# Second-half squares, row statistics and operand sums placed elsewhere at the begin of each stage of a two-layer encoder

## The chip, the cores and the metric

The kernel runs on one core of a Trainium2 chip. The metric is the device time of one execution in microseconds (us). Three runs of the kernel before are shown, and one profiled execution from which all rows below come.

## The reference

The reference is a trunk of two layers over 1024 tokens of 1024 channels in float32. Each layer has two stages that begin with a root-mean-square norm: a mixer and a feed-forward block.

```python
for l in range(DEPTH):
    h = rmsnorm(x, attn_norm_g[l])
    x = x + hybrid_mixer(h, w_in[l], ...)     # h @ w_in, then three branches, then w_out
    h = rmsnorm(x, ffn_norm_g[l])
    x = x + conv_ffn(h, w_up[l], ffn_conv_w[l], w_down[l])
return rmsnorm(x, final_norm_g)
```

What matters here is the first product of each stage: the normed `h` times a wide matrix, `w_in` (6912 columns) or `w_up` (4096 columns). A norm needs, for each token, the sum over all channels of x squared; its inverse root scales the token, and a gain scales the channel.

## The kernel before

**Layout.** Channels lie on the 128 partitions, tokens along a row. The activations come in two halves of 512 tokens; each half is four tiles (parts 0 to 3), and a tile holds two pieces of 128 x 512: channel block k and block k + 4. The first half's tiles are `x_i_0_j` at the first stage and `x_o_0_0_j` at the second, the second half's `x_i_1_j` and `x_o_0_1_j`, with j the part. Two flat operations on a piece (512 elements a partition) are the unit of almost all of VectorE's and ScalarE's work.

**Products.** Each float32 operand is held as a high and a low piece in a shorter format: ScalarE casts the high one, VectorE subtracts it from the operand for the low one. For weights that is `split_to` (L287, L288), for activations `halves` (L346, L347). A product of 128 x 128 weights and 512 tokens is then three matmuls (high by high, high by low, low by high), all at L337. Tiles `split_n` come from a pool of five buffers, so a weight cast waits until the matmuls of the weights five places back are over. Sums of weight quarters (`s1` to `s4`) are made by DMAs ahead of time and split in the same way.

**Blocks.** A `Block` makes two output tiles of 128 channels by 1024 tokens with seven products in place of eight, by sums of quarters. With b11 and b21 the first half's channel blocks 0 to 3 and 4 to 7, and b12 and b22 the second half's, the operands of activations are B11 = b11, B21 = b21, t3 = b12 - b22 (T3), T1 = b11 - b12, T2 = t3 - b11, T4 = b21 + T2, and B22 = b22. Each has four parts of 128 channels, and a product with one operand is twelve matmuls. `first()` makes B11 into the bank `run` (copied by ScalarE to p1, L381) and B21 into the bank `c11`, and VectorE adds both to z1 (L363). `second()` adds T2's product to `run`, which ScalarE copies to u2 (L391). `rest()` makes T3's product in the bank `c21`, which ScalarE copies to p7 (L401); then T1's on top of `run`, T4's on top of `c21` (so not before p7 is copied), and B22's on top of `run`.

**A stage's begin.** Four times (m_0, f_0, m_1 and f_1: mixer and feed-forward block of layers 0 and 1) `start_phase` begins a stage. Four blocks run their `first()` from the first half alone. Meanwhile the second half's row statistics are made: the sum of squares (squares by ScalarE, L477; sums by VectorE, L363), a product with ones (`st`, L422), the power on GpSimd (L429), a diagonal on VectorE (L439) and its product with ones (`r`, L452). Then VectorE norms the second half's eight pieces (L485) and makes t3, T1 and T2 in place; T2's and T3's pieces are cast and split; the four blocks run their `second()`; and T1, T4 and B22 follow. At m_0 alone there is nothing ahead of the begin: x is loaded, the first half's squares summed and its tiles normed, while the second half's tiles land. At the other three the last product of the stage before runs meanwhile.

**What sets the order.** The kernel is traced from the top, and a scheduler of the framework, when the program is built, places the instructions of every engine by its own estimate of when each can run. What the kernel text fixes is the order of what depends on each other, and `tc.issue_after(ins)`, which puts the instructions traced inside the block behind `ins` on the engine of `ins`. On the chip, every engine takes its rows in the built order, and a row that waits holds what stands behind it.

Of the kernel before, what the change touches and what calls it, by code (L numbers as in the profile page):

```python
# [10 lines left out]
AF = mybir.ActivationFunctionType  # L11
ALU = mybir.AluOpType

P = 128
D = 1024
S = 1024
L = 2
H = 512
NH = S // H
DB = 768  # L20
KD = D // P
# [51 lines left out]
C_NG = C_PS + KB  # L73
# [29 lines left out]
def encoder(ctx: ExitStack, tc: tile.TileContext, xt, wts, par, bs, wst, cnt, out):  # L103
    nc = tc.nc
# [9 lines left out]
    def slot(name):  # L114

        return up.tile([P, 2, H], F32R, tag="u", name=name)
# [5 lines left out]
    def temp(name):  # L122
        return wp.tile([P, H], F32, tag="t", name=name, bufs=N_TT)
# [63 lines left out]
    state = {"raw": 0, "split": 0, "used": 0, "dma": None, "credit": 0, "pow": None}  # L187
# [156 lines left out]
    def halves(u, f):  # L344

        nc.scalar.copy(u[:, 0], f)  # L346
        nc.vector.tensor_tensor(u[:, 1], f, u[:, 0].bitcast(F32), op=ALU.subtract)  # L347

    def split_slot(name, f):
        u = slot(name)  # L350
        halves(u, f)
        return u
# [7 lines left out]
        nc.vector.tensor_tensor(u[:, 1], whole_of(u), u[:, 0].bitcast(F32), op=ALU.subtract)  # L360

    def add(o, a, b, op=ALU.add):
        nc.vector.tensor_tensor(o, a, b, op=op)  # L363

    class Block:

# [80 lines left out]
    def rsqrt_rows(parts_of, name):  # L447

        dg, nc_ = parts_of
        r = pst.tile([P, H], F32, tag="st", name=f"r_{name}")  # L450
        for j in range(2):
            nc.tensor.matmul(r[:, :nc_], ones_r, dg[:, j, :nc_], start=j == 0, stop=j == 1)  # L452
        return r
# [17 lines left out]
    def x_part(xq, k):  # L471
        return xq[k % 4][:, k // 4]

    def square(sq, xq, k, cols, name):

        s = temp(f"sq_{name}_{k}")
        nc.scalar.activation(s[:, cols], x_part(xq, k)[:, cols], AF.Square)  # L477
        if sq is None:
            return s
        add(sq[:, cols], sq[:, cols], s[:, cols])  # L480
        return sq

    def normed_tile(xq, r, l, col, k):
        f = x_part(xq, k)
        nc.vector.scalar_tensor_tensor(  # L485
            f, f, parts[l][:, col + k : col + k + 1], r, op0=ALU.mult, op1=ALU.mult
        )

    def normed(xq, r, l, col):
        for k in range(KD):  # L490
            normed_tile(xq, r, l, col, k)
# [10 lines left out]
    def start_phase(l, col, x0, x1, sq1, name, ops, blocks, late):  # L502


        at = 2 if late else 1
        for b in blocks[:at]:
            b.first()
        rows = rsqrt_sums(sq1, 0, H, D, f"{name}_1")
        blocks[at].first()
        r = rsqrt_rows(rows, f"{name}_1")  # L510
        for b in blocks[at + 1 :]:
            b.first()
        t3 = []
        ops["T2"] = []
        for j in range(4):
            b11, b12, b22 = x_part(x0, j), x_part(x1, j), x_part(x1, j + 4)
            for k in (j, j + 4):
                normed_tile(x1, r, l, col, k)
            t3.append(temp(f"t3_{name}_{j}"))
            add(t3[j], b12, b22, ALU.subtract)  # L520
            add(b12, b11, b12, ALU.subtract)
            add(b11, t3[j], b11, ALU.subtract)
            ops["T2"].append(split_slot(f"T2_{name}_{j}", b11))
        ops["T3"] = [split_slot(f"T3_{name}_{j}", t3[j]) for j in range(4)]
        for b in blocks:
            b.second()
        ops["T1"] = [split_slot(f"T1_{name}_{j}", x_part(x1, j)) for j in range(4)]
        ops["T4"] = []
        for j in range(4):
            b21 = x_part(x0, j + 4)  # L530
            add(b21, b21, x_part(x0, j))
            ops["T4"].append(split_slot(f"T4_{name}_{j}", b21))
        ops["B22"] = [split_slot(f"B22_{name}_{j}", x_part(x1, j + 4)) for j in range(4)]
# [38 lines left out]
    def mixer_in(l, x0, x1, sq1, ops):  # L572
# [96 lines left out]
        def block(n):  # L669
            kind, j = IN_BLOCKS[n]  # L670
            return Block(l, *in_tiles(kind, j), ops, f"{kind}_{tag}_{j}")
# [26 lines left out]
                    nc.sync.dma_start(d[kind][c], z)  # L698

        blocks = [block(n) for n in range(EARLY)]  # L700
        start_phase(l, C_NG, x0, x1, sq1, f"m_{l}", ops, blocks, l == 0)
        for n in range(len(IN_BLOCKS)):
            if n >= EARLY:

                rate = PUMP[0] if n < len(IN_BLOCKS) - 6 else LAST_PUMP
                b = block(n)
# [7 lines left out]
            else:  # L714
                b, rate = blocks[n], PUMP[0]
# [224 lines left out]
        return x0, x1, sq1, ops  # L940

    def first_half(l, col, x0, sq0, name):
        normed(x0, rsqrt_rows(rsqrt_sums(sq0, 0, H, D, f"{name}_0"), f"{name}_0"), l, col)
        return first_operands(x0, name)


# [138 lines left out]
    x0 = x_load(xt, 0, "i_0", gated=False)  # L1085
    nc.sync.dma_start(parts[0], par[0])
    load_to(3)
    x1 = x_load(xt, 1, "i_1", gated=False)
    warm = sm.tile([P, 1], F32, tag="warm", name="warm", bufs=1)
    nc.scalar.activation(warm, ones[:, 0:1], AF.Sigmoid)  # L1090
    sq0 = sq1 = None
    for k in range(KD):
        sq0 = square(sq0, x0, k % 2 * 4 + k // 2, slice(0, H), "m_0_0")
    ops = first_half(0, C_NG, x0, sq0, "m_0")
    for k in range(KD):
        sq1 = square(sq1, x1, k % 2 * 4 + k // 2, slice(0, H), "m_0_1")
    later.append(lambda: nc.sync.dma_start(cnt_sb, cnt))
    for l in range(1, L):
        later.append(lambda l=l: nc.sync.dma_start(parts[l], par[l]))
    for l in range(L):  # L1100
        x_src = xt if l == 0 else x_dram[2 * l - 1]
        d = mixer_in(l, x0, x1, sq1, ops)
        x0, x1, sq1, ops = mixer_out(l, d, x_src, x_dram[2 * l])
        if l + 1 < L:
            x0, x1, sq1, ops = ffn(l, x0, x1, sq1, ops, x_dram[2 * l], x_dram[2 * l + 1])
# [96 lines left out]
```

## Time and profile before

| | |
|---|---|
| median of three runs (lowest, highest) | 2721.48 us (2721.25, 2721.61) |
| the profiled execution's own time | 2721.56 us |
| its span | 2719.7 us |
| mean granted TensorE clock | 0.998 |
| TensorE (PE) busy | 2671.9 us, 98% |
| TensorE's weight loads (PEld) busy | 2206.4 us, 81% |
| VectorE (DVE) busy | 2058.4 us, 76% |
| ScalarE (ACT) busy | 1254.6 us, 46% |
| GpSimd (POOL) busy | 370.2 us, 14% |

A row of a time line has the start in us from the span's begin, the duration from the first to the last of the instructions it merges, the engine, the line of the kernel, the operation, the tile written and those read, the size, and how often; in brackets the idle time before it and what ended it. Buffer numbers are left out of tile names there: `x_o` stands for all tiles of both halves, `T_f` for T1 to T4 at f_0 and f_1, `c_up` for c11 and c21, `run_up` for the bank `run`, `z_up` and `upv` for a block's two outputs, `p_up` for p1 and p7. A row of waits has the engine and its operation, what it waited for, the total, the number of times and the longest. A row of windows has the stretch, then busy time and number of instructions for PE, PEld, DVE, ACT and POOL, the granted share of TensorE's clock, the mean busy share of the DMA engines and what they moved.

### The profile page before, as it was taken

How to read it: one execution, taken by the hardware profiler on the slowest of the kernel's cores; microseconds unless marked ns; L12 is line 12 of the kernel's file. 1: busy time of each engine (PE TensorE's matmuls, PEld its weight loads, DVE VectorE, ACT ScalarE, POOL GpSimd, SP SyncE). 2: the span in 40 equal slices, each digit the busy share in tenths (PEclk: the TensorE clock that was granted, in tenths of full speed). 3: DMA queues.
4: the chain of work that ended last, by engine and by line, in shares of the span. 5: the costliest groups of instructions: out<-in, count | busy, mean ns of one | idle time of the engine just before them, and what ended most of it. 6: DMA issues, size and time to landing. Idle time of an engine off the chain costs nothing.

```text
span 2719.7 us, 35012 instructions
## 1 busy us (share of the span) xinstructions
PE 2671.9 (98%) x12122; PEld 2206.4 (81%) x12122; DVE 2058.4 (76%) x2879; ACT 1254.6 (46%) x2047; POOL 370.2 (14%) x423
## 2 busy tenths in 40 slices
PE   6999999999999999999999999999999999999998
PEld 4888888888888788878888888888888888888788
DVE  7997998967756976664579988898776579666656
ACT  5645444444333554553355444444442336445434
POOL 3231112100001311100122211110000022211000
PEclk9999999999999999999999999999999999999999
DMA  9888878673357787656569778786624677774654
GB/s 241 200 221 209 214 196 215 174 267 139 122 184 201 174 204 182 164 195 204 150 154 223 202 209 225 199 208 225 217 92 142 217 177 183 194 186 112 218 180 136
DMA packets 273923, 513.72 MB, mean 189 GB/s; under 512 B 28368, under 2 KB 49616, under 8 KB 273744
## 3 DMA queue, kind: packets, MB, share of 16 engines
q1 hardware_dynamic: 219120, 411.32, 45.7%
q0 software_dynamic: 54624, 100.16, 22.4%
q8 instruction: 95, 1.56, 0.2%
q14 instruction: 84, 0.69, 0.1%
HBM read 383.44 MB, written 87.03 MB: 173 GB/s over the span
## 4 chain that ended last, share of the span: by engine, by line
PE 81%; issue 13%; DVE 3%; DMA 2%; ACT 1%; POOL 0%; SPq 0%; DVEq 0%; POOLq 0%; ACTq 0%
PE run_up L337 13%; PE pd L337 12%; PE run_gate L337 10%; PE c_up L337 9%; PE c_gate L337 7%; PE run_glu L337 5%; PE ph L337 4%; PE c_glu L337 4%; PE po L337 3%; PE run_zp L337 2%; PE run_u L337 2%; PE run_v L337 2%; PE c_u L337 2%; PE c_zp L337 2%; PE c_v L337 1%
## 5 line engine op out<-in xcount | busy, mean ns | idle before, releaser
L288 DVE TENSOR_TENSOR split<-raw,split 128x512 fp32r<-128x512 f32 (+1 forms) x570 | 376.6, 665 | 254.5 <-ACT split L287 251.3
L287 ACT CAST split<-raw 128x512 fp32r<-128x512 f32 (+1 forms) x570 | 342.8, 603 | 465.1 <-PE pd L337 146.1
L595 DVE SCALAR_TENSOR_TENSOR conv<-z_glu,par,conv 128x1011 f32<-128x1011 f32 (+7 forms) x360 | 452.5, 1264 | 7.3 <-ACT conv L593 4.5
L287 ACT CAST split<-s 128x512 fp32r<-128x512 f32 x344 | 213.5, 622 | 368.6 <-issue 127.2
L337 PE MATMUL pd<-h,split 128*128 128x512 f32 (+1 forms) x1536 | 314.7, 364 | 3.7 <-ACT split L287 1.5
L337 PEld LDWEIGHTS pd<-h,split 128*128 128x128 f32 x1536 | 262.2, 189 | 51.9 <-ACT h L359 3.5
L288 DVE TENSOR_TENSOR split<-s,split 128x512 fp32r<-128x512 f32 x344 | 235.1, 686 | 65.0 <-ACT split L287 64.6
L219 POOL DMA_DIRECT2D s<-in_wts_dram x220 | 205.9, 977 | 400.0 <-DMA s<-in_wts_dram 182.2
L219 POOL DMA_DIRECT2D s<-s x156 | 136.7, 876 | 765.3 <-DMA s<-in_wts_dram 409.4
L337 PE MATMUL run_up<-T_f,split 128*128 128x512 f32 x768 | 184.5, 389 | 2.5 <-ACT T_f L346 2.5
L337 PE MATMUL run_up<-B_f,split 128*128 128x512 f32 x768 | 183.4, 393 | 2.5 <-DVE upv L363 2.5
L337 PE MATMUL c_up<-T_f,split 128*128 128x512 f32 x768 | 183.8, 389 | 0.3 <-ACT p_up L401 0.3
L337 PE MATMUL po<-y,split 128*128 128x512 f32 x768 | 175.7, 389 | 0.0
L337 PEld LDWEIGHTS run_up<-B_f,split 128*128 128x128 f32 x768 | 144.2, 189 | 34.8 <-DVE upv L363 4.7
L337 PEld LDWEIGHTS run_up<-T_f,split 128*128 128x128 f32 x768 | 143.8, 188 | 33.4 <-ACT T_f L346 3.5
L337 PEld LDWEIGHTS c_up<-T_f,split 128*128 128x128 f32 x768 | 144.0, 188 | 31.1 <-ACT p_up L401 1.2
L337 PEld LDWEIGHTS po<-y,split 128*128 128x128 f32 x768 | 144.0, 188 | 29.8
L337 PE MATMUL c_gate<-T_m,split 128*128 128x512 f32 x576 | 138.6, 389 | 0.0
L337 PE MATMUL run_gate<-T_m,split 128*128 128x512 f32 x576 | 138.5, 389 | 0.0
L337 PE MATMUL run_gate<-B_m,split 128*128 128x512 f32 x576 | 136.3, 389 | 0.0
L337 PE MATMUL ph<-mixed,split 128*128 128x512 f32 x576 | 136.1, 394 | 0.0
L337 PE MATMUL ph<-us,split 128*128 128x512 f32 x576 | 134.2, 391 | 0.0
(265 smaller groups left out, 4375.2 us busy)
## 6 DMA issues: line engine op xcount, KB each, us to landing
raw<-in_wts_dram SPq DMA_DIRECT2D x518, 256.0 KB, 3.4
s<-in_wts_dram SPq DMA_DIRECT2D x344, 256.0 KB, 3.6
s<-in_wts_dram POOLq DMA_DIRECT2D x220, 256.0 KB, 5.2
s<-s POOLq DMA_DIRECT2D x156, 256.0 KB, 4.2
gate<-z_gate SPq DMA_DIRECT2D x48, 512.0 KB, 4.2
gt<-gate SPq DMA_DIRECT2D x96, 256.0 KB, 3.7
h<-hd SPq DMA_DIRECT2D x56, 256.0 KB, 4.9
pooled_b<-poold SPq DMA_DIRECT2D x24, 512.0 KB, 10.0
```

What stands on the lines that cost most here:

```text
L219: nc.gpsimd.dma_start(s, o, accum_op=ALU.add)
L287: nc.scalar.copy(s[:, 0, :cols], src[:, :cols])
L288: nc.vector.tensor_tensor(s[:, 1, :cols], src[:, :cols], s[:, 0, :cols].bitcast(F32), op=ALU.subtract)
L337: nc.tensor.matmul(ps[:, cols], w[:, i0, wsl], a[:, i1, cols], start=first and k == 0 and j == 0, stop=last and k == n - 1 and j == 2, ski ...
L595: nc.vector.scalar_tensor_tensor(acc[:, k:], ain[:, : S - k], col(w0 - k), acc[:, k:], op0=ALU.mult, op1=ALU.add,)
```

## The change

Three edits, none of which changes what is computed.

- At m_0 the second half's squares are traced ahead of the first half's norm, and the first half's normed tiles are issued behind the sixth square on ScalarE and behind the fifth sum on VectorE (`issue_after(seen[0])`, `issue_after(seen[1])`).
- At m_0 the second half's statistics are traced behind the first block (`late` is now False), as at the other begins; it was behind the second block.
- At all four begins the second half's operand sums are made part by part: VectorE's rows of part j + 1 (two normed tiles, t3, T1, T2 and T2's low piece) are issued behind part j's last difference, T2's.

```diff
--- before.py
+++ after.py
@@ -360,7 +360,7 @@
         nc.vector.tensor_tensor(u[:, 1], whole_of(u), u[:, 0].bitcast(F32), op=ALU.subtract)
 
     def add(o, a, b, op=ALU.add):
-        nc.vector.tensor_tensor(o, a, b, op=op)
+        return nc.vector.tensor_tensor(o, a, b, op=op)
 
     class Block:
 
@@ -474,10 +474,10 @@
     def square(sq, xq, k, cols, name):
 
         s = temp(f"sq_{name}_{k}")
-        nc.scalar.activation(s[:, cols], x_part(xq, k)[:, cols], AF.Square)
+        state["squared"] = nc.scalar.activation(s[:, cols], x_part(xq, k)[:, cols], AF.Square).ins
         if sq is None:
             return s
-        add(sq[:, cols], sq[:, cols], s[:, cols])
+        state["summed"] = add(sq[:, cols], sq[:, cols], s[:, cols]).ins
         return sq
 
     def normed_tile(xq, r, l, col, k):
@@ -512,15 +512,20 @@
             b.first()
         t3 = []
         ops["T2"] = []
+        behind = None
         for j in range(4):
             b11, b12, b22 = x_part(x0, j), x_part(x1, j), x_part(x1, j + 4)
-            for k in (j, j + 4):
-                normed_tile(x1, r, l, col, k)
-            t3.append(temp(f"t3_{name}_{j}"))
-            add(t3[j], b12, b22, ALU.subtract)
-            add(b12, b11, b12, ALU.subtract)
-            add(b11, t3[j], b11, ALU.subtract)
-            ops["T2"].append(split_slot(f"T2_{name}_{j}", b11))
+
+            with ExitStack() as order:
+                if behind is not None:
+                    order.enter_context(tc.issue_after(behind))
+                for k in (j, j + 4):
+                    normed_tile(x1, r, l, col, k)
+                t3.append(temp(f"t3_{name}_{j}"))
+                add(t3[j], b12, b22, ALU.subtract)
+                add(b12, b11, b12, ALU.subtract)
+                behind = add(b11, t3[j], b11, ALU.subtract).ins
+                ops["T2"].append(split_slot(f"T2_{name}_{j}", b11))
         ops["T3"] = [split_slot(f"T3_{name}_{j}", t3[j]) for j in range(4)]
         for b in blocks:
             b.second()
@@ -698,7 +703,7 @@
                     nc.sync.dma_start(d[kind][c], z)
 
         blocks = [block(n) for n in range(EARLY)]
-        start_phase(l, C_NG, x0, x1, sq1, f"m_{l}", ops, blocks, l == 0)
+        start_phase(l, C_NG, x0, x1, sq1, f"m_{l}", ops, blocks, False)
         for n in range(len(IN_BLOCKS)):
             if n >= EARLY:
 
@@ -940,7 +945,9 @@
         return x0, x1, sq1, ops
 
     def first_half(l, col, x0, sq0, name):
-        normed(x0, rsqrt_rows(rsqrt_sums(sq0, 0, H, D, f"{name}_0"), f"{name}_0"), l, col)
+        if not isinstance(sq0, tuple):
+            sq0 = rsqrt_sums(sq0, 0, H, D, f"{name}_0")
+        normed(x0, rsqrt_rows(sq0, f"{name}_0"), l, col)
         return first_operands(x0, name)
 
 
@@ -1091,9 +1098,15 @@
     sq0 = sq1 = None
     for k in range(KD):
         sq0 = square(sq0, x0, k % 2 * 4 + k // 2, slice(0, H), "m_0_0")
-    ops = first_half(0, C_NG, x0, sq0, "m_0")
+    rows0 = rsqrt_sums(sq0, 0, H, D, "m_0_0")
+    seen = None
     for k in range(KD):
         sq1 = square(sq1, x1, k % 2 * 4 + k // 2, slice(0, H), "m_0_1")
+        if k == KD - 3:
+            seen = state["squared"], state["summed"]
+
+    with tc.issue_after(seen[0]), tc.issue_after(seen[1]):
+        ops = first_half(0, C_NG, x0, rows0, "m_0")
     later.append(lambda: nc.sync.dma_start(cnt_sb, cnt))
     for l in range(1, L):
         later.append(lambda l=l: nc.sync.dma_start(parts[l], par[l]))
```

The built order, at the three places that the prediction speaks of. First VectorE at f_0, just ahead of the first T2 product. `x_o_0_0_j` is part j of the first half, `x_o_0_1_j` of the second; a normed tile is at L485, `z1_up_0_2` and `z1_up_0_3` are outputs of the third and fourth block, `split` rows are weights. Before:

```order
L485 SCALAR_TENSOR_TENSOR x_o_0_1_2_6965<-x_o_0_1_2_6965,par_0_78,r_f_0_1_7465 128x512
L363 TENSOR_TENSOR z1_up_0_2_7468<-c11_up_0_2_7489,p1_up_0_2_7487 128x512
L288 TENSOR_TENSOR split_283_7536<-s2_0_92_7267,split_283_7536 128x512
L485 SCALAR_TENSOR_TENSOR x_o_0_1_3_6967<-x_o_0_1_3_6967,par_0_78,r_f_0_1_7465 128x512 x2
L363 TENSOR_TENSOR t3_f_0_0_7554<-x_o_0_1_0_6961 128x512
L363 TENSOR_TENSOR t3_f_0_1_7563<-x_o_0_1_1_6963 128x512
L363 TENSOR_TENSOR x_o_0_1_0_6961<-x_o_0_0_0_6634,x_o_0_1_0_6961 128x512
L363 TENSOR_TENSOR x_o_0_1_1_6963<-x_o_0_0_1_6636,x_o_0_1_1_6963 128x512
L363 TENSOR_TENSOR x_o_0_0_0_6634<-t3_f_0_0_7554,x_o_0_0_0_6634 128x512
L363 TENSOR_TENSOR z1_up_0_3_7516<-c11_up_0_3_7535,p1_up_0_3_7533 128x512
L363 TENSOR_TENSOR x_o_0_0_1_6636<-t3_f_0_1_7563,x_o_0_0_1_6636 128x512
L347 TENSOR_TENSOR T2_f_0_0_7558<-x_o_0_0_0_6634,T2_f_0_0_7558 128x512
```

The sixth to eighth normed tile are shown and the first five stand above them: all eight come ahead of the first t3. With the change, from T2's difference of part 0 on:

```order
L363 TENSOR_TENSOR x_o_0_0_0_6634<-t3_f_0_0_7554,x_o_0_0_0_6634 128x512
L485 SCALAR_TENSOR_TENSOR x_o_0_1_1_6963<-x_o_0_1_1_6963,par_0_78,r_f_0_1_7465 128x512
L363 TENSOR_TENSOR z1_up_0_3_7516<-c11_up_0_3_7535,p1_up_0_3_7533 128x512
L347 TENSOR_TENSOR T2_f_0_0_7558<-x_o_0_0_0_6634,T2_f_0_0_7558 128x512
L485 SCALAR_TENSOR_TENSOR x_o_0_1_1_6963<-x_o_0_1_1_6963,par_0_78,r_f_0_1_7465 128x512
L288 TENSOR_TENSOR split_285_7627<-s3_0_88_7492,split_285_7627 128x512
L363 TENSOR_TENSOR t3_f_0_1_7563<-x_o_0_1_1_6963 128x512
L363 TENSOR_TENSOR x_o_0_0_0_6634<-x_o_0_0_0_6634 128x512
L363 TENSOR_TENSOR x_o_0_1_1_6963<-x_o_0_0_1_6636,x_o_0_1_1_6963 128x512
L363 TENSOR_TENSOR x_o_0_0_1_6636<-t3_f_0_1_7563,x_o_0_0_1_6636 128x512
L485 SCALAR_TENSOR_TENSOR x_o_0_1_2_6965<-x_o_0_1_2_6965,par_0_78,r_f_0_1_7465 128x512 x2
L347 TENSOR_TENSOR T2_f_0_1_7567<-x_o_0_0_1_6636,T2_f_0_1_7567 128x512
```

Part 0 runs to its end first; part 1's normed tiles, its t3 and its differences stand behind part 0's last difference and around `z1_up_0_3`, the T4 sum of part 0 (`x_o_0_0_0<-x_o_0_0_0`) among them, and part 2 begins behind part 1.

The second place is ScalarE at f_0, ahead of the copy p7 of the first block. Before:

```order
L346 CAST T1_f_0_2_7686<-x_o_0_1_2_6965 128x512
L346 CAST T1_f_0_3_7689<-x_o_0_1_3_6967 128x512
L346 CAST T4_f_0_0_7693<-x_o_0_0_0_6634 128x512
L346 CAST T4_f_0_1_7697<-x_o_0_0_1_6636 128x512
L346 CAST T4_f_0_2_7701<-x_o_0_0_2_6638 128x512
L287 CAST split_288_7722<-s4_0_88_7494 128x512
L401 COPY p7_up_0_0_7737<-c21_up_0_0_7721 128x512
```

Seven casts (four of T1, of which the first two stand above the cut, and three of T4) come ahead of the split of `s4` and the copy. With the change:

```order
L346 CAST T1_f_0_3_7689<-x_o_0_1_3_6967 128x512
L346 CAST T4_f_0_0_7693<-x_o_0_0_0_6634 128x512
L346 CAST T4_f_0_1_7697<-x_o_0_0_1_6636 128x512
L346 CAST T4_f_0_2_7701<-x_o_0_0_2_6638 128x512
L346 CAST T4_f_0_3_7705<-x_o_0_0_3_6640 128x512
L346 CAST B22_f_0_0_7708<-x_o_0_1_0_6961 128x512
L346 CAST B22_f_0_1_7711<-x_o_0_1_1_6963 128x512
L346 CAST B22_f_0_2_7714<-x_o_0_1_2_6965 128x512
L346 CAST B22_f_0_3_7717<-x_o_0_1_3_6967 128x512
L287 CAST split_288_7722<-s4_0_88_7494 128x512
L401 COPY p7_up_0_0_7737<-c21_up_0_0_7721 128x512
```

The fourth cast of T4 and the four of B22 have moved ahead of the split and the copy (the first three casts of T1 stand above the cut).

The third place is VectorE at m_0, where the first half's pieces are normed (`x_i_0_j`; `sq_m_0_1_0` is the second half's sum of squares). Before:

```order
L439 TENSOR_TENSOR dg_m_0_0_156<-ident_84,rp_m_0_0_153 128x512 x2
L288 TENSOR_TENSOR split_2_284<-raw_2_109,split_2_284 128x512
L485 SCALAR_TENSOR_TENSOR x_i_0_0_96<-x_i_0_0_96,par_0_78,r_m_0_0_159 128x512
L485 SCALAR_TENSOR_TENSOR x_i_0_1_98<-x_i_0_1_98,par_0_78,r_m_0_0_159 128x512
L485 SCALAR_TENSOR_TENSOR x_i_0_2_100<-x_i_0_2_100,par_0_78,r_m_0_0_159 128x512
L485 SCALAR_TENSOR_TENSOR x_i_0_3_102<-x_i_0_3_102,par_0_78,r_m_0_0_159 128x512
L485 SCALAR_TENSOR_TENSOR x_i_0_0_96<-x_i_0_0_96,par_0_78,r_m_0_0_159 128x512
L485 SCALAR_TENSOR_TENSOR x_i_0_1_98<-x_i_0_1_98,par_0_78,r_m_0_0_159 128x512
L485 SCALAR_TENSOR_TENSOR x_i_0_2_100<-x_i_0_2_100,par_0_78,r_m_0_0_159 128x512
L485 SCALAR_TENSOR_TENSOR x_i_0_3_102<-x_i_0_3_102,par_0_78,r_m_0_0_159 128x512
L347 TENSOR_TENSOR B11_m_0_0_170<-x_i_0_0_96,B11_m_0_0_170 128x512
```

The eight normed tiles followed the third weight split at once. With the change:

```order
L288 TENSOR_TENSOR split_2_284<-raw_2_109,split_2_284 128x512
L363 TENSOR_TENSOR sq_m_0_1_0_159<-sq_m_0_1_0_159,sq_m_0_1_4_161 128x512
L363 TENSOR_TENSOR sq_m_0_1_0_159<-sq_m_0_1_0_159,sq_m_0_1_1_164 128x512
L363 TENSOR_TENSOR sq_m_0_1_0_159<-sq_m_0_1_0_159,sq_m_0_1_5_167 128x512
L363 TENSOR_TENSOR sq_m_0_1_0_159<-sq_m_0_1_0_159,sq_m_0_1_2_170 128x512
L363 TENSOR_TENSOR sq_m_0_1_0_159<-sq_m_0_1_0_159,sq_m_0_1_6_173 128x512
L485 SCALAR_TENSOR_TENSOR x_i_0_0_96<-x_i_0_0_96,par_0_78,r_m_0_0_182 128x512
L363 TENSOR_TENSOR sq_m_0_1_0_159<-sq_m_0_1_0_159,sq_m_0_1_3_176 128x512
L485 SCALAR_TENSOR_TENSOR x_i_0_1_98<-x_i_0_1_98,par_0_78,r_m_0_0_182 128x512
L363 TENSOR_TENSOR sq_m_0_1_0_159<-sq_m_0_1_0_159,sq_m_0_1_7_179 128x512
L485 SCALAR_TENSOR_TENSOR x_i_0_2_100<-x_i_0_2_100,par_0_78,r_m_0_0_182 128x512
L485 SCALAR_TENSOR_TENSOR x_i_0_3_102<-x_i_0_3_102,par_0_78,r_m_0_0_182 128x512
```

Five sums of the second half's squares now stand between the split and the first normed tile, and one more behind each of the first two normed tiles.

## The prediction

> **What bounds the kernel now.** I read the page's busy shares first, then TensorE's waits, then the time lines of the stretches in which those waits lie.
>
> ```profile
> span 2719.7 us, 35012 instructions
> PE 2671.9 (98%) x12122; PEld 2206.4 (81%) x12122; DVE 2058.4 (76%) x2879; ACT 1254.6 (46%) x2047; POOL 370.2 (14%) x423
> ...
> PE st_m L422 <- DVE sq_m L363: 13.5, 1, 13.5
> PE run_glu L337 <- ACT T_m L346: 4.6, 3, 2.1
> PE r_m L452 <- DVE dg_m L439: 3.4, 2, 2.7
> PE run_up L337 <- DVE upv L363: 2.5, 2, 2.1
> PE run_up L337 <- ACT T_f L346: 2.5, 2, 1.2
> ```
>
> TensorE is busy 98% of the span, so a change of order shifts the end only by the TensorE idle time it makes or removes. Outside the first 13.5 us little is there to remove: 4.6 and 2.5 us before the T2 products, 3.4 us before the rows' statistics. What could be added is larger, and one view tells why. These are the stretches from the first T2 product to the first T4 product of the first block, at the second stage's begin (f_0) and at the first's (m_0):
>
> ```profile
> core 0: us, PE busy (x) PEld busy (x) DVE busy (x) ACT busy (x) POOL busy (x), PEclk, DMA share, GB/s
> 902.78:919.62 16.84, 16.67 (x72) 13.34 (x72) 16.84 (x29) 11.73 (x23) 3.72 (x5) 1.00 0.66 130
> ...
> 54.01:73.67 19.66, 17.46 (x72) 13.20 (x72) 19.66 (x33) 11.72 (x23) 6.36 (x8) 1.00 0.78 154
> ```
>
> VectorE is busy for 16.84 of 16.84 us there, beside a TensorE with 16.67. It has no slack where the change puts its rows. And f_0 is dense only because VectorE begins it with a stock, all eight normed tiles and two differences done:
>
> ```profile
> 898.68 2.88 PE L337 MATMUL c_up<-B_f,split 128*128 128x512 f32 x12
> 902.78 11.23 PE L337 MATMUL run_up<-T_f,split 128*128 128x512 f32 x48 [1.23 <-ACT T_f L346]
> 913.86 2.88 PE L337 MATMUL c_up<-T_f,split 128*128 128x512 f32 x12
> 916.58 2.88 PE L337 MATMUL run_up<-T_f,split 128*128 128x512 f32 x12
> 919.63 2.58 PE L337 MATMUL c_up<-T_f,split 128*128 128x512 f32 x10 [0.17 <-ACT p_up L401]
> ```
>
> The 48 T2 products run without a gap, T3 and T1 follow, and T4 begins 16.85 us after T2. One product takes (916.58 - 913.86)/12 = 0.227 us.
>
> **The parts in order, T2 (f_0; m_1 and f_1 have the same orders).** VectorE's and ScalarE's rows there:
>
> ```profile
> 896.15 0.69 DVE L363 TENSOR_TENSOR z_up<-c_up,p_up 128x512 f32<-128x512 f32 x1
> 897.42 1.40 DVE L485 SCALAR_TENSOR_TENSOR x_o<-x_o,par,r_f 128x512 f32<-128x512 f32 x2
> 901.75 0.68 DVE L363 TENSOR_TENSOR z_up<-c_up,p_up 128x512 f32<-128x512 f32 x1
> 902.95 0.68 DVE L347 TENSOR_TENSOR T_f<-x_o,T_f 128x512 fp32r<-128x512 f32 x1
> 915.69 4.30 DVE L347 TENSOR_TENSOR T_f<-x_o,T_f 128x512 fp32r<-128x512 f32 x7
> ```
> ```profile
> 899.36 0.63 ACT L287 CAST split<-s 128x512 fp32r<-128x512 f32 x1
> 901.59 0.62 ACT L287 CAST split<-s 128x512 fp32r<-128x512 f32 x1 [1.61 <-PE c_up L337]
> 902.12 0.61 ACT L346 CAST T_f<-x_o 128x512 fp32r<-128x512 f32 x1
> 911.84 1.08 ACT L391 COPY u_up<-run_up 128x512 f32<-128x512 f32 x2
> 914.32 0.61 ACT L391 COPY u_up<-run_up 128x512 f32<-128x512 f32 x1
> 914.80 3.77 ACT L346 CAST T_f<-x_o 128x512 fp32r<-128x512 f32 x7
> 918.45 0.64 ACT L287 CAST split<-s 128x512 fp32r<-128x512 f32 x1
> 918.97 0.60 ACT L401 COPY p_up<-c_up 128x512 f32<-128x512 f32 x1
> ```
>
> VectorE's step from row to row is (4.30 - 0.68)/6 = 0.603 us for a sum, 0.66 for a normed tile (1.40 - 0.74); ScalarE's is (3.77 - 0.62)/6 = 0.525. An operand is out 0.68 or 0.62 after its row's start; 0.03 to 0.05 us go to the next engine.
>
> The start of T2 does not move. T2's first cast stands on ScalarE behind the fifth weight cast, which waits for c_up's end (901.59, 1.61 us waited), so TensorE still starts at 902.78. What the change gives up is the stock: by then VectorE used to have eight normed tiles; now every row of part 1 stands behind part 0's last difference. That stands behind the weight split of 899.36 (cast over at 899.99), so it starts at 900.60; one normed tile goes at 901.20, z_up at 901.86. Queued behind them are T2's low part (902.77, its cast ends at 902.73) and part 1: second normed tile 903.37, a weight split 904.03, t3 904.63, the T4 sum 905.24, two differences 905.84 and 906.44. The cast runs from 907.16 to 907.78, TensorE gets part 1 at 907.83. Its twelve products of part 0 ended at 902.78 + 2.72 = 905.50: a new wait of 2.33 us.
>
> Each further part costs VectorE two normed tiles and five sums (low part, t3, T4 sum, two differences): 2 x 0.66 + 5 x 0.603 = 4.34 us, against 2.72 for the twelve products. Parts 2 and 3 so begin at 912.17 and 916.51, and T2 ends at 919.23 where it was 913.86: **+5.37 us**. From below: nothing, if VectorE found time ahead of 902.78, but it stands twice for ScalarE and TensorE there, as the rows say. From above: 4 x 4.34 less 11.08, which is +6.3.
>
> **The parts in order, T4.** Four blocks now take a part in turn and end T2 within four products, so ScalarE cannot copy u_up early: behind T2's last cast (915.84) and the four of T3 the first copy starts at 915.84 + 5 x 0.525 = 918.46, 0.8 us ahead of T2's end (911.84 was 2.0 ahead). Four copies and two splits later (6 x 0.525) the casts of T1 begin at 921.61. Then the second shift: because the T4 sums are made early, ScalarE's order now has all twelve casts of T1, T4 and B22 ahead of the split and the copy p_up; it had seven. T4's products add to the bank that p_up must have read. So p_up starts at 921.61 + 13 x 0.525 = 928.43 and T4 at 929.08, 9.85 us behind T2's end instead of 5.77: **+4.1 us**, of it 2.6 from five more casts. TensorE waits some 3.5 us in one piece for p_up. T3 and T1 hide the rest. From below 0 if the casts went on another engine, which the order excludes; from above +4.8 with TensorE's restart and T1's own wait counted twice.
>
> T2 and T4 together: +9.45 us, three times: **+28.4**.
>
> **m_0.** The rows of the very begin:
>
> ```profile
> 10.28 3.08 DVE L363 TENSOR_TENSOR sq_m<-sq_m,sq_m 128x512 f32<-128x512 f32 x4 [1.21 <-ACT sq_m L477]
> 18.56 0.68 DVE L288 TENSOR_TENSOR split<-raw,split 128x512 fp32r<-128x512 f32 x1
> 19.53 5.36 DVE L485 SCALAR_TENSOR_TENSOR x_i<-x_i,par,r_m 128x512 f32<-128x512 f32 x8 [0.28 <-PE r_m L452]
> 24.80 4.90 DVE L347 TENSOR_TENSOR B_m<-x_i,B_m 128x512 fp32r<-128x512 f32 x8
> 25.54 4.97 PE L337 MATMUL run_glu<-B_m,split 128*128 128x512 f32 x11 [0.60 <-DVE B_m L347]
> 40.10 0.95 PE L422 MATMUL st_m<-ones,sq_m 128*128 128x1 f32 x8
> 41.70 2.91 PE L337 MATMUL c_v<-B_m,split 128*128 128x512 f32 x12
> 45.25 1.10 PE L452 MATMUL r_m<-dg_m,ones_r 128*128 128x512 f32 x2 [0.63 <-DVE dg_m L439]
> 48.94 2.89 PE L337 MATMUL c_v<-B_m,split 128*128 128x512 f32 x12
> 54.01 0.50 PE L337 MATMUL run_glu<-T_m,split 128*128 128x512 f32 x1 [1.74 <-ACT T_m L346]
> ```
>
> Sums that need the one before step by (3.08 - 0.69)/3 = 0.80. After the split of 18.56 five such sums now precede the first normed tile: 19.16 + 4 x 0.80 + 0.60 = 22.96 instead of 19.53. Two more stand between the tiles: the eighth ends its step at 22.96 + 8 x 0.66 + 2 x 0.603 = 29.45, where the low parts began at 24.80: +4.65. The dense products so start at 30.19 instead of 25.54. Of the loss comes back: two first products that go ahead of that point (0.45); the statistics' products st_m, now in idle time (0.9); r_m's wait, since its sums are complete by 26 and no longer at 40 (from c_v's end at 41.70 + 2.72 = 44.42 to the twelve products ahead of 48.94, at 46.22, are 1.80, of which r_m's two need 0.46: 1.34); T2's first cast, which no longer stands behind an activation (51.66 to 54.01 is 2.35, at f_0 901.40 to 902.78 is 1.38: 0.97). So T2 begins at 54.01 + 4.65 - 3.66 = 55.0. From there to T4 it takes the 26.3 us of f_0's walk (929.08 - 902.78), against 19.66 before: in all **+7.6 us**. The squares moved on ScalarE lie in its wait for the first normed tile; the three issues on SP that trade places, and two on POOL, carry pieces which are cast only for T1 to B22, long behind: nothing.
>
> Sum: 28.4 + 7.6 = +36.0 us on the profiled 2721.56 (its span 2719.7 plus 1.9 around it; the median of the runs shown is 2721.48).
>
> **The clock.** The long waits have a second price, which two windows show:
>
> ```profile
> 1183.70:1187.50 3.80, 1.75 (x7) 1.06 (x7) 3.80 (x7) 3.80 (x8) 0.00 (x0) 0.99 0.92 337
> 1187.50:1190.50 3.00, 3.00 (x8) 2.34 (x7) 2.84 (x5) 0.35 (x1) 0.00 (x0) 0.50 0.32 115
> ```
>
> After the 2.1 us wait for upv the granted clock was 0.50 for 3 us, 8 products instead of 13: some 1.4 us lost. The equal wait of 2.1 us at T_m had no such sequel (granted 1.00 in its window above). The new waits of 3.5 us, one a stage, are longer than either. I price two of the four at 1.4 to 1.6: +3, with 0 and 6.4 as ends. T2's own waits cost no more by it, since TensorE has 1.6 us in hand per part.
>
> [...]
>
> **Forecast:** 2721.56 + 36.0 + 3 = **2760.6 us**, 1.4% slower.
>
> **The rivals.**
>
> - *The clock takes all.* Each of the four long waits and some at T2 bring a window at 0.50, eight in all at 1.5 us: 2721.56 + 36.0 + 12 = 2769.6. For it: the waits come close together. Against it: one such window in the whole trace of before, behind two waits over 2 us.
> - *T4 is not late.* If the copy p_up finds T3's bank early enough, or the casts run ahead of my walk, T4's term goes and with it the long waits: 36.0 - 4 x 4.1 = 19.6, so 2741. For it: p_up's wait is 0.17 us today. Against it: ScalarE takes rows in order, and twelve casts stand ahead.
> - *Not slower.* The parts are ready in time: VectorE does part 0 and 1 while TensorE is in c_up of the last two blocks, so T2 stays dense, and only m_0's early statistics count: 4.65 - 3.66 - (19.66 - 16.84) = -1.8, so 2720. It decides if VectorE gets 4.34 us per part ahead of 902.78. Against it: z_up, behind which part 1 stands, needs c_up's last product.
> - *The order doesn't bind.* The built order shows the rows moved at all four begins, so this has no chance worth a number.
>
> **How the numbers follow.** The forecast has 0.68, the clock 0.14, T4 in time 0.13, not slower 0.05. The forecast's own ends are 36.0 - 6 (a part's step 0.3 shorter, T1's waits hidden) and 36.0 + 6.4: 2751 to 2764. Half of the clock's case is let in: 2750 to 2767 leaves out the rest of it, T4 in time, and not slower, about two in ten. No change means within 0.2% (5.4 us), what can be told here: faster 0.01, the same 0.04, slower 0.95.
>
> **What would show it.** Right: T2's 48 products at f_0 span 16.4 us in four groups with waits for T_f near 2.3, 1.3 and 1.3 us; T4 waits about 3.5 us for p_up; r_m of m_0 has no wait; the first dense products start near 30.2. Wrong: T2 dense, or T4 right behind T1. The forecast fails as a whole if VectorE is idle inside these stretches without waiting for ScalarE.

## The result, and the profile after

The changed kernel takes 2760.34 us (median of four runs, 2758.20 to 2763.91), the kernel before 2721.36 beside it: ratio 1.0146, 95% interval 1.0131 to 1.0160, so 39.0 us slower. The profiled execution took 2762.2 us, 40.6 more than that of before.

The page's head and TensorE's waits of the changed kernel:

```profile
span 2760.4 us, 34998 instructions
PE 2687.3 (97%) x12122; PEld 2214.4 (80%) x12122; DVE 2064.9 (75%) x2879; ACT 1255.5 (45%) x2047; POOL 363.1 (13%) x423
...
PE run_up L337 <- ACT T_f L346: 10.0, 7, 2.2
PE run_glu L337 <- ACT T_m L346: 9.2, 7, 2.1
PE c_up L337 <- ACT p_up L401: 6.4, 2, 3.2
PE c_glu L337 <- ACT p_glu L401: 6.3, 2, 3.2
PE run_glu L337 <- ACT B_m L346: 4.9, 1, 4.9
```

The work is the same, 12122 matmuls. Before, the waits for T_f and T_m were 2.5 and 4.6 us in total, and T4's waits for p_up and p_glu 0.17 us each at three of the begins, with none at m_0; now there are four of 3.2 us, one a begin. Each stands ahead of the first block's T4 products, as TensorE's time line at f_0 shows:

```profile
906.22 2.88 PE L337 MATMUL c_up<-B_f,split 128*128 128x512 f32 x12
910.33 3.01 PE L337 MATMUL run_up<-T_f,split 128*128 128x512 f32 x12 [1.23 <-ACT T_f L346]
915.50 3.39 PE L337 MATMUL run_up<-T_f,split 128*128 128x512 f32 x12 [2.16 <-ACT T_f L346]
919.95 3.38 PE L337 MATMUL run_up<-T_f,split 128*128 128x512 f32 x12 [1.07 <-ACT T_f L346]
924.40 3.02 PE L337 MATMUL run_up<-T_f,split 128*128 128x512 f32 x12 [1.07 <-ACT T_f L346]
927.26 2.88 PE L337 MATMUL c_up<-T_f,split 128*128 128x512 f32 x12
...
930.71 2.79 PE L337 MATMUL run_up<-T_f,split 128*128 128x512 f32 x11 [0.23 <-DVE T_f L347]
936.70 4.21 PE L337 MATMUL c_up<-T_f,split 128*128 128x512 f32 x12 [3.19 <-ACT p_up L401]
```

T2, one group of 48 before, is four groups with a wait ahead of each; T3 and T1 follow, and T4 (936.70) stands 936.70 - 910.33 = 26.37 us behind T2's begin instead of 16.85. VectorE sets the groups' pace, one part from a second normed tile to the next:

```profile
914.71 1.40 DVE L485 SCALAR_TENSOR_TENSOR x_o<-x_o,par,r_f 128x512 f32<-128x512 f32 x2
...
917.84 0.68 DVE L363 TENSOR_TENSOR x_o<-x_o,x_o 128x512 f32<-128x512 f32 x1
918.55 0.69 DVE L363 TENSOR_TENSOR x_o<-t_f,x_o 128x512 f32<-128x512 f32 x1
919.16 1.40 DVE L485 SCALAR_TENSOR_TENSOR x_o<-x_o,par,r_f 128x512 f32<-128x512 f32 x2
```

At the dots stand T2's low piece, t3 and the T4 sum. No row waits, so that a part takes 919.16 - 914.71 = 4.45 us. ScalarE's rows ahead of the copy p7 (p_up):

```profile
929.29 4.28 ACT L346 CAST T_f<-x_o 128x512 fp32r<-128x512 f32 x8
933.46 2.19 ACT L346 CAST B_f<-x_o 128x512 fp32r<-128x512 f32 x4
935.53 0.63 ACT L287 CAST split<-s 128x512 fp32r<-128x512 f32 x1
936.05 0.59 ACT L401 COPY p_up<-c_up 128x512 f32<-128x512 f32 x1
```

ScalarE is never idle from 929.29 on: twelve casts, a split, then the copy, while T3's bank has been ready since 927.26 + 2.72 = 929.98.

The third loss is the clock. These are the windows of the 24 products from T4 on at the four begins (f_0, m_0, m_1, f_1), then of T2 at f_0 and at f_1:

```profile
936.70:943.92 7.22, 7.22 (x25) 5.74 (x26) 4.93 (x8) 2.12 (x4) 2.18 (x3) 0.76 0.58 158
78.81:87.24 8.43, 8.43 (x24) 6.66 (x25) 4.93 (x8) 3.40 (x5) 1.79 (x3) 0.64 0.60 156
1437.74:1445.98 8.24, 8.24 (x25) 6.53 (x26) 4.93 (x8) 3.41 (x5) 2.65 (x3) 0.66 0.62 160
2296.28:2303.44 7.16, 7.16 (x25) 5.74 (x26) 4.93 (x8) 2.12 (x4) 2.00 (x3) 0.76 0.58 163
910.33:927.26 16.93, 12.50 (x48) 8.73 (x49) 16.79 (x27) 4.76 (x9) 3.51 (x4) 1.00 0.60 114
2269.92:2286.85 16.93, 13.63 (x49) 9.92 (x50) 16.79 (x27) 4.78 (x9) 3.50 (x4) 0.90 0.59 111
```

24 products at full clock are 24 x 0.227 = 5.4 us; they take 7.2 to 8.4 at a granted clock of 0.64 to 0.76, behind all four waits. T2 is different: with a half-clock window inside (0.90) or none (1.00) it spans the same 16.93 us, since VectorE paces it.

### The profile page after: what moved, and what is told of

It reads as the page before. It is cut to its first block, busy times and chain, and to the rows that moved or that the text cites. A ratio compares the mean times of both kernels' runs of the same rounds, so it can differ in the third digit from the quotient of the medians.

```text
span 2760.4 us, 34998 instructions
## 1 busy us (share of the span) xinstructions
PE 2687.3 (97%) x12122; PEld 2214.4 (80%) x12122; DVE 2064.9 (75%) x2879; ACT 1255.5 (45%) x2047; POOL 363.1 (13%) x423
## 4 chain that ended last, share of the span: by engine, by line
PE 78%; issue 13%; DVE 4%; ACT 3%; DMA 2%; POOL 0%; SPq 0%; DVEq 0%; POOLq 0%; ACTq 0%
PE pd L337 12%; PE run_up L337 11%; PE run_gate L337 9%; PE c_up L337 9%; PE c_gate L337 7%; PE run_glu L337 4%; PE ph L337 4%; PE c_glu L337 4%; PE po L337 3%; PE run_zp L337 2%; PE run_u L337 2%; PE run_v L337 2%; PE c_zp L337 2%; PE c_u L337 2%; PE c_v L337 2%
```

## The experiments

The theory had three parts: T2 is late by VectorE's work per part once the stock of normed tiles is gone; T4 is late by the casts ahead of p7 on ScalarE; the clock falls behind the long waits. The main rival was one cause: VectorE makes T2 late, and T4 follows from that. All ratios are against the kernel before.

**The edits apart.** e1 leaves m_0 as before and keeps the part order; e2 does the reverse.

```diff
# e1_parts_only: from the changed kernel
-        start_phase(l, C_NG, x0, x1, sq1, f"m_{l}", ops, blocks, False)
+        start_phase(l, C_NG, x0, x1, sq1, f"m_{l}", ops, blocks, l == 0)
...
-    rows0 = rsqrt_sums(sq0, 0, H, D, "m_0_0")
-    seen = None
+    ops = first_half(0, C_NG, x0, sq0, "m_0")
...
-    with tc.issue_after(seen[0]), tc.issue_after(seen[1]):
-        ops = first_half(0, C_NG, x0, rows0, "m_0")
# e2_m0_only: from the changed kernel
-                if behind is not None:
-                    order.enter_context(tc.issue_after(behind))
```

> Only the third edit is kept (operand sums part by part at all four begins); at m_0 the squares, the first half's normed tiles and the late statistics are as before. Theory (two queues: T2 is late by VectorE's work per part, T4 by the casts ahead of p7 on ScalarE): f_0, m_1 and f_1 are as in the changed kernel, and at m_0 the first dense products start 4.65 us earlier but the 3.66 us of idle time won by the early squares are lost, so the time is that of the changed kernel less 1.0: 2759.4 us, 2755 to 2763. T4 waits about 3.2 us for p_up or p_glu four times. Rival (the early squares are a loss of their own that is not won back): 4.65 us less, 2755.7, with m_0's T2 starting 4 us earlier than in the changed kernel.

> Only the first two edits are kept (m_0's squares ahead of the first half's normed tiles, statistics behind the first block); the operand sums are made in the old order. Theory: +4.65 at the first dense products, -3.66 by idle time used, and m_0's T2 to T4 falls from 19.66 to f_0's 16.84 (-2.8), since the stock of normed tiles is there in time: -1.8 us, 2719.6, and f_0, m_1, f_1 unchanged. Rival (the early squares' delay is not won back): +4.65 or, with the stock, +1.8, so 2723.2 to 2726.

e1: 2759.97 us, 1.0139 (1.0124 to 1.0154): the part order alone makes the whole loss. The rival's 2755.7 us is too near to be excluded by that time; the trace excludes it, since from the first statistics product to m_0's T2 are 54.06 - 13.84 = 40.22 us in e1 and 52.44 - 12.29 = 40.15 in the changed kernel, where the rival had e1 4 us earlier. e2: 2717.80 us, 0.9987 (0.9978 to 0.9997): faster by some 3 us, so the early squares are no loss of their own, and a little better than the theory's 1.8. At m_0 T2 begins about as late as before (54.01), but the stock is there, in e2's time line:

```profile
53.42 0.50 PE L337 MATMUL run_glu<-T_m,split 128*128 128x512 f32 x1 [1.68 <-ACT T_m L346]
...
70.14 2.47 PE L337 MATMUL c_glu<-T_m,split 128*128 128x512 f32 x10
```

From T2 to T4 are 16.72 us instead of 19.66. So the change held a small gain at m_0, which its own third edit took back.

**The two queues apart.** e3 moves the casts of T4 and B22 behind the first block's p7; e5 takes the normed tiles out of the part order; e7 does both.

```diff
# e3_p7_first: in start_phase, called by the first block's rest() with its copy p7
-            ops["T4"].append(split_slot(f"T4_{name}_{j}", b21))
-        ops["B22"] = [split_slot(f"B22_{name}_{j}", x_part(x1, j + 4)) for j in range(4)]
+        def last_operands(p7):
+            with tc.issue_after(p7):
+                for j in range(4):
+                    ops["T4"].append(split_slot(f"T4_{name}_{j}", x_part(x0, j + 4)))
+                ops["B22"] = [split_slot(f"B22_{name}_{j}", x_part(x1, j + 4)) for j in range(4)]
# e5_norms_free
+            for k in (j, j + 4):
+                normed_tile(x1, r, l, col, k)
             with ExitStack() as order:
                 if behind is not None:
                     order.enter_context(tc.issue_after(behind))
-                for k in (j, j + 4):
-                    normed_tile(x1, r, l, col, k)
```

> The changed kernel with one difference: the casts and low parts of T4 and B22 stand behind the first block's copy p7, so that four casts (T1's) stand ahead of it and not twelve. Theory: T2 stays 16.9 us in four groups; p7 starts eight casts (4.2 us) earlier, so T4's wait of 3.2 us falls below 0.6 at all four begins; since the eight casts now stand ahead of the second block's weight casts, up to 1.5 us a begin come back there. 4 x (3.2 - 1.4) = 7 us less by the waits alone, 2753; with the half-clock windows behind those waits (7.9 us lost in the changed kernel's trace) gone too, 2745. Rival (T4 is late because T2 is late, VectorE being the one limit): T4's low parts arrive no earlier, the wait stays near 3 us and the time near 2760.

> The changed kernel with the normed tiles taken out of the part order: only t3, the two differences and T2's low piece of a part stand behind the part before. Theory: the stock of normed tiles is back, a part costs VectorE five sums (5 x 0.603 and 0.12 for a dependent pair, 3.1 us) against TensorE's 2.72, so T2 spans 12 to 13 us instead of 16.9; T4 still waits some 3.2 us for p_up, since the twelve casts ahead of p7 are untouched. 4 x 4.3 = 17 us less: 2743 us, 2738 to 2748. Rival 1 (T4 is late only because T2 is): the wait goes too, and the clock windows with it, 2721 to 2727. Rival 2 (VectorE's sum of work to T4 is what counts): T4 waits 4 us longer, the time stays near 2760.

> The changed kernel with both mends: the normed tiles out of the part order (as in e5) and the casts of T4 and B22 behind the first block's copy p7 (as in e3); m_0's first two edits stay. Theory (two separate queues, whose losses add): e5 took 17.5 us off and e3 took 13.2, together 30.7, so 2729.6 us, 2726 to 2733; T2 spans 12.8 us, T4 waits under 0.6 us, and what stays over the kernel before are T2's last 1.7 us and the second block's wait for its weights. Rival (both mends use up the same slack on ScalarE, so that the second gives less where the first is in): 2735 to 2742.

e3: 2747.17 us, 1.0091 (1.0074 to 1.0108), 13.2 less than the changed kernel. Its f_0, with ScalarE's copy and then TensorE's rows:

```profile
930.77 0.60 ACT L402 COPY p_up<-c_up 128x512 f32<-128x512 f32 x1
```
```profile
909.21 3.01 PE L337 MATMUL run_up<-T_f,split 128*128 128x512 f32 x12 [1.23 <-ACT T_f L346]
...
926.16 2.88 PE L337 MATMUL c_up<-T_f,split 128*128 128x512 f32 x12
...
932.22 3.27 PE L337 MATMUL c_up<-T_f,split 128*128 128x512 f32 x12
936.10 0.73 PE L337 MATMUL c_up<-T_f,split 128*128 128x512 f32 x2 [0.61 <-ACT split L287]
```

T2 is as late as ever (926.16 - 909.21 = 16.95), yet T4 has no wait: T4's lateness is not T2's. The eight casts now delay the second block's weights, as expected (0.61 us there).

e5: 2742.81 us, 1.0074 (1.0059 to 1.0089), 17.5 less. The opposite picture at f_0:

```profile
906.80 3.02 PE L337 MATMUL run_up<-T_f,split 128*128 128x512 f32 x12 [1.23 <-ACT T_f L346]
910.01 3.29 PE L337 MATMUL run_up<-T_f,split 128*128 128x512 f32 x12 [0.20 <-ACT T_f L346]
...
919.62 2.88 PE L337 MATMUL c_up<-T_f,split 128*128 128x512 f32 x12
...
929.06 5.49 PE L337 MATMUL c_up<-T_f,split 128*128 128x512 f32 x12 [3.17 <-ACT p_up L401]
```

With the stock back, T2 spans 12.82 us, and T4 waits 3.17 us all the same. Both rivals fall: VectorE's lateness neither causes T4's nor is handed on to it.

e7: 2733.77 us, 1.0044 (1.0030 to 1.0057), 26.6 less; the sum of the two would be 30.7. The expected range ended at 2733 and the rival's began at 2735, so the time alone decides for neither.

```profile
902.97 3.02 PE L337 MATMUL run_up<-T_f,split 128*128 128x512 f32 x12 [1.23 <-ACT T_f L346]
...
921.89 3.22 PE L337 MATMUL c_up<-T_f,split 128*128 128x512 f32 x12
```

At the begin itself the two add: T2 to T4 is 26.37 in the changed kernel, 23.01 in e3, 22.26 in e5, so 18.90 for both, and 921.89 - 902.97 = 18.92 is measured. The other three begins agree with their sums as closely. What is missing lies elsewhere in the run. TensorE's waits for upv and for h (the operand of the down product), far from any begin, were in e7:

```profile
PE run_up L337 <- DVE upv L363: 2.8, 2, 2.0
...
PE pd L337 <- ACT h L359: 2.3, 3, 1.8
```

In the changed kernel, e3 and e5 they were 1.8, 2.1 and 0.9 for upv and 3.0, 1.5 and 0.6 for h. If savings added there too, e7 would have 2.1 + 0.9 - 1.8 = 1.2 and none; it has 1.6 and 2.3 more, which is nearly the 4.1 us missing. But these waits differ by as much between kernels that have nothing changed there: for upv 1.4 in e2 and 3.1 in e9, for h 2.1 in e2 and 0.4 in e8. So what is missing is no sign that the two mends share a limit; whether the medians lack 4.1 us for this reason alone is not shown.

**The clock apart.** e4 puts twelve products that nobody reads into the wait for p7, between T1's and T4's; e6 puts four or eight.

```diff
# e4_fill_wait, in rest() behind T1's products (first block of a stage)
+                with tc.issue_after(behind):
+                    bank = pst.tile([P, H], F32, tag="st", name=f"fill_{self.name}")
+                    for k in range(self.fill):
+                        idle = nc.tensor.matmul(
+                            bank, ones_r, ops["T1"][k % 4][:, 0], start=True, stop=True
+                        ).ins
...
# e6_fill_4, e6_fill_8
-FILL = 12
+FILL = 4    # or 8
```

> The changed kernel with twelve products more at each of the four begins, into a bank that nobody reads (so they compute nothing that is used): they stand on TensorE between the first block's T1 and T4 products and fill 12 x 0.227 = 2.7 us of the 3.2 us in which T4 waits for p7. Nothing else moves. Theory (the wait has a second price, half-clock windows that follow it; in the changed kernel's trace the products at half clock behind the four T4 waits lost 2.6, 1.6, 2.4 and 1.4 us, together 7.9): those windows go, T4 starts when it did, 2760.3 - 7.9 = 2752.4 us, 2749 to 2756. The half-clock windows inside T2 may stay and cost nothing, since T2 is paced by VectorE. Rival (the waits alone make the loss and the clock windows come anyhow, or their loss is made up later): 2760, 2757 to 2764.

> As e4_fill_wait, with four products in the place of twelve (they compute nothing that is used): 4 x 0.227 = 0.9 us of the 3.2 us wait for p7 are filled, 2.3 us stay. It asks how long a wait must be to bring a half-clock window behind it. Theory (a wait of 2.1 to 2.3 us is enough in part of the cases, as at T2 and at upv): windows behind about two of the four T4 waits at 1.6 us each, 2753.7 + 3.2 = 2757 us, 2755 to 2759. Rival 1 (a wait must come near 3 us): no window at T4, 2753.7, as with twelve. Rival 2 (any wait over 2 us brings them): as the changed kernel, 2760.

> As e4_fill_wait, with eight products in the place of twelve (they compute nothing that is used): 1.8 us of the 3.2 us wait are filled, 1.4 us stay. Theory: 1.4 us is below the waits that brought a window so far, so none at T4 and 2753.7 us, 2752 to 2756. Rival (what counts is the share of idle time in a stretch of 3.4 us, the products of T1 with their own wait of 0.23 included): one or two windows, 2755 to 2757.

e4: 2753.71 us, 1.0119 (1.0105 to 1.0133): more work on TensorE, and 6.6 us less; its slowest run (2755.56) is faster than the fastest of the changed kernel (2758.20). Its windows, the 24 products from T4 on at f_0 and m_0:

```profile
936.01:941.62 5.61, 5.61 (x24) 4.61 (x25) 4.87 (x8) 2.13 (x4) 0.79 (x2) 1.00 0.43 141
...
80.13:85.74 5.61, 5.61 (x26) 4.61 (x25) 4.87 (x8) 3.41 (x5) 0.90 (x2) 1.00 0.45 145
```

Full clock, 5.61 us. Against it the changed kernel's four stretches lose 7.22 + 8.43 + 8.24 + 7.16 - 4 x 5.61 = 8.6 us in the profiled execution. With eight fillers it took 2752.82 us (1.0118, 1.0103 to 1.0133), which is e4's time within 0.9 us, as the theory had it. With four it took 2757.43 us (1.0145, 1.0125 to 1.0166; one run of 2766 makes it wide), which can be told neither from the changed kernel nor from e4; in its trace half clock came behind the T4 wait of m_1 and not behind that of f_0, where the theory had two of the four. With four, m_1 waited less than f_0, since four transposes of 0.6 us in all stand there too, and it was m_1 that lost clock:

```profile
1433.43 4.50 PE L339 MATMUL c_glu<-T_m,split 128*128 128x512 f32 x12 [1.81 <-ACT p_glu L405]
...
934.64 3.06 PE L339 MATMUL c_up<-T_f,split 128*128 128x512 f32 x12 [2.24 <-ACT p_up L405]
```

That is 4.50 us for twelve products behind a wait of 1.81, and 3.06 behind 2.24, so here the length of the wait did not tell. Its place in time differed. In the traces of the kernel before and of the changed one the granted clock is recorded as changing 20 times, 4 and 16; the first is at 30.28 us in both, and each of the other 18 comes a whole multiple of 3.413 us behind it (57.59, 61.00, 78.07, 84.89 and 938.23 us in the changed kernel, 1187.40 and 1190.81 in the one before). These are stretches of that length in e6_fill_4, around m_1's wait and f_0's:

```profile
1431.21:1434.62 3.41, 1.60 (x9) 1.19 (x8) 3.41 (x7) 3.41 (x8) 0.00 (x0) 1.00 0.15 26
1434.62:1438.03 3.41, 3.41 (x10) 2.63 (x9) 1.85 (x4) 0.38 (x2) 0.00 (x0) 0.50 0.57 169
...
932.86:936.27 3.41, 1.63 (x7) 1.35 (x8) 3.41 (x6) 3.29 (x7) 0.00 (x0) 1.00 0.02 5
936.27:939.68 3.41, 3.41 (x17) 2.80 (x16) 3.26 (x6) 0.62 (x1) 0.14 (x1) 1.00 0.66 199
```

The wait of 1.81 us lies whole in one window, and the next has half clock; of the 2.24 us only 1.78 lie in one, and the next has full clock. In the traces of before and of the changed kernel, two of the twelve, from the first recorded change to 15 us before the end, eight windows of that length between those multiples had full clock with 1.88 to 2.95 us of idle TensorE, and half clock followed in all eight; the other windows at full clock had 1.74 or less, and none was followed by it. Of the ten windows at half clock, a second one followed the two that had 0.74 and 1.16 us of idle time themselves, and none of the eight with 0.08 or less: the wait of m_0 had 2.44 us ahead of a window's end and 0.74 behind it, that of m_1 1.97 and 1.16, and both brought two, while those of f_0 (1.88 ahead) and f_1 (2.95) brought one. That is what these two traces show; where the boundary lies, they do not. e6_fill_8's rival, the share of idle time in a stretch of 3.4 us, thus agrees with them in kind, though its one or two windows are not in the time; T4's waits there were 1.32 us at most.

**Better than both?** e9 is e2 without `issue_after(seen[...])`, so that sums and normed tiles alternate on VectorE; e8 adds eleven unread products in m_0's idle time.

```diff
# e9_squares_free: from e2
-    with tc.issue_after(seen[0]), tc.issue_after(seen[1]):
-        ops = first_half(0, C_NG, x0, rows0, "m_0")
+    ops = first_half(0, C_NG, x0, rows0, "m_0")
# e8_squares_free_warm: from e9
+    for k in range(FILL):
+        nc.tensor.matmul(warm_bank, ones_r, ops["B11"][0][:, 0], start=True, stop=True)
```

> The kernel before with m_0's second half's squares traced ahead of the first half's norm and the statistics behind the first block, but the normed tiles are not held behind any square; the sums of squares and the normed tiles alternate on VectorE, so that no sum waits for the one before (step 0.60 and not 0.80); no part order. Theory: the kernel with the first two edits alone (2717.8) less some of 5 x 0.2 = 1.0 us: 2717.0, 2715 to 2719, against 2720.9 before. Rival (the dense products still start at the same place, and T2's begin hangs on TensorE's products alone): no better than 2717.8.

> As e9_squares_free, with eleven products more at m_0 into a bank that nobody reads (nothing computed from them is used), in TensorE's idle time ahead of the first half's products. Theory of the clock: the half-clock window at the first dense products (1.2 to 2.0 us lost in the traces so far) goes: 2715.5 to 2716. Rival: a window comes by the idle times that stay (0.5 to 1.4 us between the first products), no difference to e9.

e9: 2718.64 us, 0.9992 (0.9983 to 1.0001); e8: 2718.34, 0.9989 (0.9980 to 0.9998). Neither gains on e2, and e8's expectation was missed. The products at m_0 become dense no earlier in e9 (29.81 us) than in e2 (29.42). In e8's trace the first eleven dense products did take 2.82 us in place of e9's 5.04, but a window at half clock inside T2 then took 1.6 us back, and the medians show no gain. So e2, the first two edits without the third, has the lowest median, and e8 and e9 can't be told from it: it is faster than the changed kernel by 42.5 us, and than the kernel before by 0.13%, which is less than the 0.2% that one measurement can tell and rests on the interval of ten runs.

## Why the prediction was right

It said 2760.6 us, slower, by T2 and T4 at each begin; the runs say 2760.3, by the same two places. By its own steps:

- **T2's start does not move.** Right: c_up's last product at 906.22 + 2.72 = 908.94, T2 at 910.33, 1.39 us behind, predicted 1.38.
- **T2, +5.37.** Right in kind, 0.48 too small: 927.26 - 910.33 = 16.93 against 11.08 is +5.85. A part takes 4.45 us and not 4.34: T2's difference, which overwrites the tile that the row just before it reads, starts 0.71 behind that row (917.84 to 918.55), where I used 0.603. The first part is later by the same 0.12, and the last group takes 927.26 - 924.40 = 2.86 where I used 2.72.
- **T4, +4.1.** Measured 936.70 - 927.26 = 9.44 against 5.77, +3.67. The copy itself was foreseen to 0.07 us (928.43 and the 7.55 by which all of f_0 came later is 935.98; it started at 936.05). That it came so close is in part luck: T2's last cast came 0.34 later than walked (923.73 against 915.84 + 7.55), and the rows from there to the copy made it up, since ScalarE's copies step shorter than the 0.525 that I used (926.34 to 929.29 is 2.95 for the four copies and two splits, against 3.15). T2 and T4 together: 9.52 against 9.45. e3 and e5 show that they are two causes. The wait of 3.5 us that I named is not what my walk gives: 929.08 - 919.23 less 24 x 0.227 is 4.4 us for the waits of T1 and T4 together, and 9.44 - 5.45 = 4.0 was measured, 3.19 of it ahead of T4.
- **m_0, +7.6.** About 1.2 too large. T2 to T4 grew by 26.37 - 19.66 = 6.71, as walked. But T2's start, counted from the first statistics product of each trace, came 0.35 earlier (52.44 - 12.29 against 54.01 - 13.51) instead of 1.0 later. The rows of the changed kernel:

```profile
12.29 1.84 PE L422 MATMUL st_m<-ones,sq_m 128*128 128x1 f32 x8 [12.29 <-DVE sq_m L363]
...
29.13 3.24 PE L337 MATMUL run_glu<-B_m,split 128*128 128x512 f32 x11
...
39.70 0.80 PE L452 MATMUL r_m<-dg_m,ones_r 128*128 128x512 f32 x2
...
52.44 0.50 PE L337 MATMUL run_glu<-T_m,split 128*128 128x512 f32 x1 [0.83 <-ACT T_m L346]
```

  The dense products are 4.81 later on that count (29.13 - 12.29 against 25.54 - 13.51; predicted 4.65), and the second half's r_m has no wait, as said. The term left out is that the first eleven dense products took 4.97 us before and take 3.24 here, 1.73 less. That looks like the clock too: in both traces products step by 0.427 us until 30.3 us from the span's begin and by 0.227 from then on; the record of the granted clock starts only there, but 0.427 is also their step where it shows 0.50 (1187.40 to 1190.81 before, 78.07 to 84.89 here, but for the wait). In the changed kernel only three of the eleven fall ahead of it. Where the step falls is not the kernel's doing alone: it came at 29.2 us in e1 and at 35.2 in e9, so the size of this term is in part chance.
- **The clock, +3.** The step that failed in size. I let two of the four waits for p7 lose 1.4 to 1.6 us each; all four did, two of them 1.6 us and two of them 2.6 and 2.8, which is 8.6 us in the profiled execution, and 6.6 by e4's median. In e5 the wait of 3.17 us at f_0 did so too: twelve products took 5.49 us behind it instead of 2.88. The price of one window was a little low: eight products in the place of 13 are 1.1 us and not 1.4, and the whole group behind that wait lost more, 4.53 us for twelve products instead of 2.88:

```profile
1186.19 4.53 PE L337 MATMUL run_up<-B_f,split 128*128 128x512 f32 x12 [2.05 <-DVE upv L363]
```

  Its other half held: T2's own windows cost nothing, 16.93 us with and without one.
- **The sum.** 3 x 9.52 + 6.71 - 0.35 + 8.6 = 43.5 us at the four begins, against 39.0 predicted. The profiled execution is 40.6 longer, so some 2.9 were won elsewhere: 1.2 in the first 13 us (12.29 against 13.51), and 3.6 between f_0 and the first down product, where the kernel before had the wait for upv of 2.05 us and the half clock behind it and the changed kernel had neither; some 2 us were lost again by other waits of this sort. The total came out closer than the terms did, by luck: too little for the clock was offset by too much at m_0 and by these differences.

Of the rivals, "T4 is not late" and "not slower" fall with the trace. "The clock takes all" was half right: there were eight windows at the begins, but the two inside T2 were free of charge, so that its +12 was too much and the forecast's +3 too little.

## What to carry to other kernels

Where two engines take their rows in the built order, as VectorE and ScalarE did at f_0 (twelve casts and a split, from 929.29 on, ahead of the copy at 936.05), and feed a third, an order that makes parts one after the other gives up the stock that covered the feeder's slower pace, and on the second feeder it can bring later work ahead of a copy that the third engine needs now: read what stands ahead of each awaited row, on each queue. Losses on separate queues add where they arise, and are mended separately. Price a new TensorE wait by what the traces show behind waits of its length, unless TensorE has slack there: in the changed kernel each of the four of 3.2 us at T4 had 3.41 or 6.83 us of half clock behind it, which cost 1.6 to 2.8 us.

## What the runs showed of the hardware

- In the changed kernel half clock followed each of the four waits of 3.2 us ahead of T4, for 3.41 us at f_0 and f_1 and for 6.83 us at m_0 and m_1. At T2 a wait of 2.16 us (f_0) was followed by full clock and one of 2.15 (f_1) by 3.41 us of half clock; in e6_fill_4 half clock came behind 1.81 us and not behind 2.24.
- The recorded changes of the granted clock lie whole multiples of 3.413 us behind the first of their trace (3 in the kernel before, 15 in the changed kernel), and waits of nearly equal length that lay differently between them ended differently: at T2 the 2.15 us of f_1 lay whole in one such window, while of the 2.16 us of f_0 no window had more than 1.24 us of idle time.
- The first products stepped by 0.427 us instead of 0.227: until 30.3 us from the span's begin in the kernel before and in the changed one, until 35.2 us in e9, and until 24.4 us in e8, with unread products ahead.
- Twelve unread products in each wait of 3.2 us (e4) made the program 6.6 us faster: TensorE's idle time there was dearer than its work.
- Two VectorE rows of 128 x 512 of which the second overwrites what the first reads stepped by 0.71 us in the changed kernel (917.84 to 918.55), independent ones by 0.60 (916.63 to 917.23).
